# Splitting twenty weight tiles of a recurrent mixer beside the MLP before it, and a planner that knows two-operand reads

## Chip, cores and metric

One Trainium2 chip, one core. The metric is the device time of one execution in microseconds (us); lower is better.

## What is computed

Two layers over 1024 latent tokens and 256 context tokens, width 1024: banded attention with an MLP, then a recurrent block (a gated linear recurrence in two directions) with an MLP. Cut to what the change touches, the recurrent mixer is:

```python
w_gate, w_rec = w_in[:, :D_RNN], w_in[:, D_RNN:]             # D_RNN = 1280
u_x = centred_dwconv(h_x @ w_rec, conv_w, conv_b)            # and u_c for the context tokens
for d in range(2):                                           # both directions
    a_c, bx_c = rglru_coeffs(u_c, w_a[d], b_a[d], w_i[d], b_i[d], lam[d])
    ys_c, hc_last = linear_scan(a_c, bx_c, 0, rev, ...)
    a_x, bx_x = rglru_coeffs(u_x, w_a[d], b_a[d], w_i[d], b_i[d], lam[d])
    ys_x, _ = linear_scan(a_x, bx_x, hc_last, rev, True)
y_x = (gelu(h_x @ w_gate) * (rec_x[0] + rec_x[1])) @ w_out
```

`rglru_coeffs` multiplies `u`, in five blocks of 256 columns, with `w_a` and `w_i`, and takes sigmoid, exp, tanh and a square root of the products. All is fp32.

## The kernel before

**Products.** An fp32 product is made of three fp32r matmuls (`mm3`, lines 249 to 251): each operand is split into a high half (a copy rounded to fp32r) and a low half (the fp32 value minus the high half); high x high, high x low and low x high add up in PSUM. So each weight tile of 128x1024 goes through `plan_w`: a DMA into one of three `raw` buffers, a copy for the high half on ACT or DVE (line 244), a subtraction for the low half on DVE or POOL (line 1525, two SBUF inputs), both into one of four `w` slots; then `raw` is free again. A split is named by its output: `w` for whole tiles, `hw`, `ws` and `hc` for narrower ones.

**Stages.** Attention runs to about 660 us. The first MLP follows (`layer0_mlp`): after four columns of hidden units, fourteen steps of `plan_seven` make two tiles of hidden units each with seven products instead of eight, and put them in DRAM (`hid_d`, line 1447, 256 KB each). `plan_second` then reads them back and multiplies by `w2` in eight chunks of 2, 4, 4, 4, 4, 4, 4 and 2 tiles. Beside this run the rows of the conditioning vector (`plan_ada`, line 1236). `middle` plans the last four hidden tiles, the residual with its norms, the recurrent mixer and the start of the second MLP. `plan_in` makes the products of `w_in`: ten tiles for `u` (line 1883 begins their convolution; `u` goes to DRAM), and ten gate tiles, whose products of 512 tokens each run in two passes `g`, so each gate tile is loaded and split twice (ACT takes the gelu, line 1921). `plan_rec` runs for five blocks `n` and two directions: `u` is read back and split (`uh`, `uhc`, lines 1958 to 1967), the tile `wg[n, d]` is loaded and split, products `pg` follow, sigmoids (line 2005), exp, tanh and square root on ACT, products on DVE and POOL (lines 2047 to 2079), and scans on DVE (line 2087). The two directions are added (line 2120), multiplied by the gate (line 2123), put in DRAM and read back for the product with `w_out`.

**What sets the order.** `Plan` is a list scheduler that runs when the kernel is built. Every operation has one or several engines with a duration for each, a key (lower is more urgent), dependencies, and slots that it takes and frees (`w` 4, `raw` 3, `t` 32 places of 4 KB, `s` 21 places of 2 KB). `order` simulates the engines and emits each engine's instructions in the order of simulated time; `p.any` operations may go to DVE or POOL (or ACT), to the second engine only if it would end at most `alt` ns later than the first. All DMAs of this part are issued by SP in the order of their simulated times, so a DMA that waits holds those behind it. The layer-0 MLP and `middle` are one plan, with the keys `KEYS2`; the second MLP is another, with `KEYS3`.

Of the kernel before, what the change touches and what calls it, by code (L numbers as in the profile page):

```python
# [17 lines left out]
P = 128  # L18
D = 1024
# [23 lines left out]
class Plan:  # L43
# [14 lines left out]
    def add(self, eng, ns, key, fn, deps=(), take=(), free=(), tab=None):  # L58
# [23 lines left out]
    def order(self):  # L82
# [11 lines left out]
        bus = 0.0  # L94
# [19 lines left out]
        while len(at) < len(ops):  # L114
# [84 lines left out]
class Body:  # L199
# [190 lines left out]
    def run(self):  # L390
        tc, nc, A = self.tc, self.nc, self.A
        with ExitStack() as es:
# [18 lines left out]
            self.g_d = dt([4, 2, KT, P], F32, name="g_d")  # L411

# [741 lines left out]
    def layer0_mlp(self):  # L1154
# [58 lines left out]
        for c, n in enumerate([2] + [4] * 6 + [2]):  # L1213
            last = self.plan_second(p, l, 1000 + 100 * c, m, n, c, put, last, ys, yop, yh, (8, 9, 0, 1, 2, 3, 4, 5, 6, 7), rows)
            m += n
# [39 lines left out]

    def plan_ctx(self, p, key, j, z, o, zc, put):
# [34 lines left out]
    def plan_second(self, p, l, K, m, n, c, put, last, ys, yop, yh, order, rows=None, fin=False):  # L1291
# [14 lines left out]
        for i, t in enumerate(order):  # L1306
# [12 lines left out]
            if rows is not None and n == 4 and i in (1, 2, 3, 4, 5, 7, 8):  # L1319
                rows(1, K + 2 * i, o)  # L1320
            if fin:
# [290 lines left out]
    def plan_residual(self, p, key, t, ys, yop, xs, xop, G, put, norm):  # L1612
# [25 lines left out]
        for n in range(2):  # L1638
            g.append(p.any(PAIR(512), "DVE Pool", key, lambda e, n=n: e.tensor_tensor(
                out=y(n), in0=y(n), in1=G["G"][:, n * 512:(n + 1) * 512], op=ALU.mult), [sq[n], G["op"]]))  # L1640
            o.append(p.add("DVE", 665, key, lambda n=n: nc.vector.scalar_tensor_tensor(  # L1641
                out=x(n), in0=y(n), scalar=z["a"][:, 2:3], in1=x(n), op0=ALU.mult, op1=ALU.add), [r, g[n], xop]))
# [53 lines left out]
    def middle(self, p, ys, yop, yh, hput, last):  # L1696
# [58 lines left out]
        E["dep"] = last  # L1755
# [97 lines left out]
    def plan_in(self, p, E, h, hop, hold):  # L1853
# [5 lines left out]
        for m in range(NR):  # L1859
# [38 lines left out]
            for i in (0, 1, 3):  # L1898
                o = p.add("DVE", 1200, key, lambda i=i, z=z, tap=tap: tap(i, z["x"], z["u"]), [o], free=[(es[0], 0)] if i == 3 else [])
# [33 lines left out]
    def plan_rec(self, p, E):  # L1933
# [4 lines left out]
        for n in range(NB):  # L1938
# [32 lines left out]
            for kt in range(2):  # L1971
                lu.append(p.add("DMA", 2500, K - 4, load(kt), deps, take=["t"]))
                c = p.add("DVE", 800, K - 4, split_c(kt), [luc], take=["s"])
                a = p.add("DVE", 605, K - 4, split(kt, 0), [lu[kt]], take=["t"])
                b = p.add("DVE", 1140, K - 4, split(kt, 1), [a], take=["t"])
# [3 lines left out]
            for d in range(2):  # L1979
                K = Z["c0"] + (2 * n + d) * Z["cp"]  # L1980
                w = self.plan_w(p, A["wg"][n, d], K - 4, [gpe[-Z["bg"]] if gpe else E["dep"]], "DVE ACT")
# [49 lines left out]
                for jt in range(2):  # L2031
                    for c in (1, 0):
# [28 lines left out]
                        st[jt, c] = p.add("DVE", sz * 1.04 + 70, q, f_st, [b, w_], free=[(w_, 0)])  # L2061
# [7 lines left out]
                for jt in range(2):  # L2069
                    for c in (1, 0):  # L2070
# [11 lines left out]
                        bb[jt, c] = p.add("DVE", sz * 1.04 + 70, q, f_b, [x, iu[jt, c]], free=[] if c else [own["r%d" % jt]])  # L2082
# [9 lines left out]
                    x = p.add("DVE", 600, q, f_scan(0, 256, 1), [bb[jt, 1]])  # L2092
                    if d == 0:
                        x = p.add("DVE", 2130, q, f_scan(0, D, 0), [x, bb[jt, 0]], free=[own["a%d" % jt]])
                        sc[jt] = [x, x]
                    else:
                        x = p.add("DVE", 1140, q, f_scan(512, D, 0), [x, bb[jt, 0]])
                        sc[jt] = [p.add("DVE", 1140, q, f_scan(0, 512, 0), [x], free=[own["a%d" % jt]]), x]
# [115 lines left out]
```

## Time and profile before

| | us |
|---|---|
| median of three runs (2858.09 to 2860.35) | 2858.9 |
| the profiled execution | 2859.99 |
| its span, first to last instruction | 2858.2 |
| busy in the span: PE / DVE / ACT / POOL | 2673.9 / 2127.6 / 1107.5 / 851.0 |

The profile is one execution on the chip. PE is TensorE's matmuls, PEld its weight loads, DVE is VectorE, ACT is ScalarE, POOL is GpSimd, SP issues DMAs. Busy times of matmuls overlap, so that a full PE shows as 100% and the number of matmuls in a stretch tells its speed; the clock is given as the share of 2.4 GHz that was granted, which has a level of 1.2 GHz below it. The name behind a line is the tile written and those read. A wait row reads "who waits, at which tile and line <- what came last: us in total, times, longest".

### The profile page before, as it was taken

The numbers are of one execution on the slowest core, as the hardware profiler recorded it, in microseconds if no ns is written. First come the engines' busy times: TensorE is split into PE (matmuls) and PEld (weight loads), VectorE is DVE, ScalarE is ACT, GpSimd is POOL, SyncE is SP. The second block draws the span as 40 slices with busy tenths as digits, with TensorE's granted clock in tenths as the row PEclk, the third lists the DMA queues.
The fourth block names the chain that finished last, engine by engine and source line by source line (L and its number), as shares of the span: only waits on it lengthen the run. The fifth ranks groups of instructions, "written<-read, shape, count | busy, mean of one in ns | idle before, by whom it ended". The sixth has DMA issues, their size and how long they took to land. (4 is left out here: it accounts for less than half of the span.)

```text
span 2858.2 us, 35048 instructions
## 1 busy us (share of the span) xinstructions
PE 2673.9 (94%) x12886; PEld 2205.4 (77%) x12886; DVE 2127.6 (74%) x3178; ACT 1107.5 (39%) x2040; POOL 851.0 (30%) x720
## 2 busy tenths in 40 slices
PE   6798999998999999999998999978896999999997
PEld 4677788877788888888887887756675888888886
DVE  8988999996876666765668677799988666655546
ACT  5326777775322223111115245776525212221111
POOL 7643444443311110100116022355435111101113
PEclk9899999999999999999999999988998999999999
DMA  6462321224233334454552223334331323333323
GB/s 233 157 218 83 110 78 45 68 65 163 74 121 105 129 129 159 155 169 140 168 177 81 92 78 98 136 125 155 139 112 63 110 100 111 133 126 110 102 83 125
DMA packets 115332, 345.03 MB, mean 121 GB/s; under 512 B 12836, under 2 KB 15828, under 8 KB 115160
## 3 DMA queue, kind: packets, MB, share of 16 engines
q1 hardware_dynamic: 111704, 330.21, 34.2%
q10 hardware_dynamic: 3456, 12.58, 1.1%
q8 instruction: 101, 1.65, 0.2%
q14 instruction: 71, 0.58, 0.1%
HBM read 254.37 MB, written 88.38 MB: 120 GB/s over the span
## 5 line engine op out<-in xcount | busy, mean ns | idle before, releaser
L251 PE MATMUL pf<-h,w 128*128 128x512 f32 (+1 forms) x1400 | 517.5, 370 | 23.7 <-POOL w L1525 17.4
L250 PE MATMUL pf<-h,w 128*128 128x512 f32 (+1 forms) x1400 | 516.2, 369 | 9.8 <-DVE h L1593 9.5
L249 PE MATMUL pf<-h,w 128*128 128x512 f32 (+1 forms) x1400 | 516.6, 369 | 5.5 <-ACT h L1583 2.8
L1500 DVE TENSOR_TENSOR y<-y,py 128x512 f32<-128x512 f32 x268 | 183.0, 685 | 274.4 <-PE py L251 273.8
L251 PEld LDWEIGHTS pf<-h,w 128*128 128x128 f32 x1400 | 267.8, 191 | 70.5 <-POOL w L1525 20.0
L250 PEld LDWEIGHTS pf<-h,w 128*128 128x128 f32 x1400 | 267.8, 191 | 56.2 <-DVE h L1593 13.0
L249 PEld LDWEIGHTS pf<-h,w 128*128 128x128 f32 x1400 | 268.0, 191 | 50.7 <-ACT w L244 3.3
L244 ACT CAST w<-raw 128x1024 fp32r<-128x1024 f32 x142 | 148.4, 1049 | 325.2 <-PE pf L251 107.5
L249 PE MATMUL py<-hw,hw 128*128 128x512 f32 x592 | 230.4, 389 | 0.0
L251 PE MATMUL py<-hw,hw 128*128 128x512 f32 x592 | 230.3, 389 | 0.0
L250 PE MATMUL py<-hw,hw 128*128 128x512 f32 x592 | 230.3, 389 | 0.0
L244 ACT CAST hw<-raw 128x512 fp32r<-128x512 f32 x113 | 69.2, 621 | 391.3 <-DMA raw<-in_w 154.3
L1473 POOL TENSOR_TENSOR hw<-raw,hw 128x512 fp32r<-128x512 f32 x46 | 65.3, 1422 | 489.3 <-DVE hw L244 337.9
L1003 POOL TENSOR_SCALAR P<-P,sc 128x640 f32<-128x640 f32 (+2 forms) x160 | 118.5, 753 | 179.7 <-DVE sc L1000 92.2
L249 PE MATMUL py<-w,hw 128*128 128x512 f32 x432 | 169.0, 391 | 0.0
L250 PE MATMUL py<-w,hw 128*128 128x512 f32 x432 | 168.6, 390 | 0.0
L251 PE MATMUL py<-w,hw 128*128 128x512 f32 x432 | 168.4, 390 | 0.0
L1092 PE MATMUL py<-w,oT 128*128 128x512 f32 x480 | 147.5, 412 | 2.5 <-DVE w L927 1.8
L986 ACT ACTIVATE P<-S,sc 128x640 f32<-128x640 f32 (+2 forms) x160 | 113.9, 712 | 52.8 <-DVE sc L980 35.5
L1473 DVE TENSOR_TENSOR hw<-raw,hw 128x512 fp32r<-128x512 f32 x156 | 116.5, 769 | 20.1 <-ACT hw L244 18.4
L249 PEld LDWEIGHTS py<-hw,hw 128*128 128x128 f32 x592 | 111.1, 188 | 23.2
L251 PEld LDWEIGHTS py<-hw,hw 128*128 128x128 f32 x592 | 111.1, 188 | 23.1
(297 smaller groups left out, 6412.7 us busy)
## 6 DMA issues: line engine op xcount, KB each, us to landing
raw<-in_w SPq DMA_DIRECT2D x128, 512.0 KB, 3.5
raw<-in_ada_t SPq DMA_DIRECT2D x96, 512.0 KB, 3.8
raw<-hid_d SPq DMA_DIRECT2D x64, 512.0 KB, 4.0
hid_d<-c SPq DMA_DIRECT2D x112, 256.0 KB, 2.3
raw<-in_w_in SPq DMA_DIRECT2D x30, 512.0 KB
x<-x_d SPq DMA_DIRECT2D x26, 512.0 KB, 5.6
x_d<-x SPq DMA_DIRECT2D x24, 512.0 KB, 2.8
q_d<-qd ACTq DMA_DIRECT2D x20, 512.0 KB, 4.3
```

The source lines that it names most:

```text
L244: (e.copy if e is self.nc.scalar else e.tensor_copy)(out=out, in_=x)
L249: mm(o, lhsT=lh, rhs=rh, start=start, stop=False, skip_group_check=on)
L250: mm(o, lhsT=lh, rhs=rl, start=False, stop=False, skip_group_check=on)
L251: mm(o, lhsT=ll, rhs=rh, start=False, stop=stop, skip_group_check=on)
L986: nc.scalar.activation(out=z["P"][j][:, :n], in_=z["S", j][:, 256:256 + n], func=AF.Exp, scale=0.125, bias=negm[:, j:j + 1], accum_out=l[: ...
L1003: nc.gpsimd.tensor_scalar(out=z["P"][j][:, :n], in0=z["P"][j][:, :n], scalar1=z["sc"][3][:, j:j + 1], scalar2=1.0, op0=ALU.mult, op1=ALU.mult)
L1092: nc.tensor.matmul(z["ps", n], lhsT=oT[k // 2][2]["oT"][:, x, k % 2], rhs=Wo[k][:, w, n * 512:(n + 1) * 512], start=m == 0, stop=m == 3 * ...
L1473: e.tensor_tensor(out=z[n][:, 1], in0=z["raw"][:, s], in1=z[n][:, 0].bitcast(F32), op=ALU.subtract)
L1500: nc.vector.tensor_tensor(out=y, in0=y, in1=z["ps"], op=ALU.add)
```

## The change

- A new `plan_pre` splits the ten gate tiles of `w_in` and the ten tiles of `wg` in two halves of 512 columns each: per half a DMA in, a copy on ACT, a subtraction on DVE, and two DMAs that put the halves in a new DRAM tensor `ws_d`. One tile goes with each of the fourteen `plan_seven` steps and one with each of the six chunks of four in `plan_second`. It takes three `s` places per half.
- A new `plan_split` takes the place of `plan_w` for these tiles in the mixer: one DMA of 1 MB from `ws_d` straight into a `w` slot. That is twenty loads for the gates (each tile twice) and ten for `wg`. The ten `u` tiles of `w_in` and those of `w_out`, `w1` and `w2` stay with `plan_w`.
- The planner marks operations that read two SBUF operands. If POOL runs one of them, a marked DVE operation that starts meanwhile is simulated longer, by 0.3 of what is left of POOL's time, at most 0.43 of its own. DMAs over 4000 ns count twice on the simulated bus.
- All keys of `KEYS2` have new values. The first loads of `plan_in` wait for the third `w2` split instead of a matmul; the first `wg` load waits for the store of the second `u` tile.

```diff
@@ Plan.add
+    def add(self, eng, ns, key, fn, deps=(), take=(), free=(), tab=None, two=False):
...
+        if two or many and "Pool" in eng and "DVE" in eng:
+            self.two.add(len(self.ops))
@@ Plan.order
-            f = t + dict(opts)[eng]
-            if eng == "DMA" and dict(opts)[eng] >= 2000 and self.keys.get("bus"):
-                bus = max(t, bus) + self.keys["bus"] * (1 if dict(opts)[eng] > 2300 else 0.5)
+            d = dict(opts)[eng]
+            if i in self.two and self.cal:
+                if eng == "Pool":
+                    pool = t + d
+                elif eng == "DVE" and pool > t:
+                    d += min(0.43 * d, 0.3 * (pool - t))
+            f = t + d
+            if eng == "DMA" and key > -1e8 and d >= 2000 and self.keys.get("bus"):
+                bus = max(t, bus) + self.keys["bus"] * (2 if d > 4000 else 1 if d > 2300 else 0.5)
@@ KEYS2
-    KEYS2 = dict(m=(2.3, 0.68, 10.54), p=(7.5, 1.52, 9.72), h=(10.4, 11.24, 37.3), pi=0.66, a0=28.64, ap=9.33, al=-5.36, g0=155.5,
-                 g1=151.7, gp=4.73, c0=98.5, cp=2.33, w0=312.9, wp=16.6, r0=389.52, spill=5, tab=122.87, alt=72.5, ba=8, bb=6, bw=9, bg=7,
-                 bo=0, hm=1, cal=1, bus=2300, eps=dict(DVE=20, ACT=0, Pool=48))
+    KEYS2 = dict(m=(5.15, 1.46, -2.67), p=(-0.6, 0.76, 14.46), h=(21.62, 13.09, 34.46), pi=0.48, a0=28.13, ap=2.3, al=8.9, g0=118.63, g1=190.44,
+                 gp=4.47, c0=43.61, cp=4.66, w0=278.53, wp=17.22, r0=455.78, spill=5, tab=311.53, alt=600, ba=7, bb=8, bw=15, bg=5, bo=0, hm=1, cal=1,
+                 bus=2300, eps={'DVE': 20, 'ACT': 50, 'Pool': 0})
@@ layer0_mlp (and plan_second, for chunks of four: pre(1, K + 2 * i, o) at its first token tile)
+        pre = self.plan_pre(p)
...
+            pre(1, 100 + 20.0 * q + 8, pace[-1])
@@ new functions
+    def plan_pre(self, p):
+        left = [u for i in range(NR) for u in (("g", i), ("in", i))]
...
+                    def load(pool, hi, lo, z=z, u=u, s=s, tile=tile):
+                        z["raw"], z["pools"] = tile(pool), (hi, lo)
+                        nc.sync.dma_start(out=z["raw"], in_=src[u[0]](u[1])[:, s])
...
+                        nc.scalar.copy(out=z["hi"], in_=z["raw"])
...
+                        nc.vector.tensor_tensor(out=z["lo"], in0=z["raw"], in1=z["hi"].bitcast(F32), op=ALU.subtract)
...
+                        nc.sync.dma_start(out=self.ws_d[self.pre_at[u], :, i, s], in_=z[n].bitcast(F32))
+                    r = p.add("DMA", 2300, key, load, [dep], take=["s"] * 3)
+                    a = p.add("ACT", 630, key, f_hi, [r])
+                    b = p.add("DVE", 690, key, f_lo, [a], free=[(r, 0)])
+                    ops.append(p.add("DMA", 2300, key, lambda put=put: put("hi", 0), [a, b], free=[(r, 1)]))
+                    ops.append(p.add("DMA", 2300, key, lambda put=put: put("lo", 1), [b], free=[(r, 2)]))
...
+    def plan_split(self, p, u, key, deps=()):
...
+            z["w"] = self.wp.tile([P, 2, D], F32R, tag="w", name=self.name("w"))
+            self.nc.sync.dma_start(out=z["w"].bitcast(F32), in_=self.ws_d[self.pre_at[u]])
+        z["op"] = p.add("DMA", 5000, key, load, list(deps) + self.pre_op[u], take=["w"])
@@ middle, plan_in, plan_rec
-        E["dep"] = last
+        E["dep"] = w2[HW - 1]["op"]
...
-                w = self.plan_w(p, A["w_in"][m], key - 3, [back(Z["bb"])])
+                w = self.plan_split(p, ("in", m), key - 3, [back(Z["bb"])])
...
-                w = self.plan_w(p, A["wg"][n, d], K - 4, [gpe[-Z["bg"]] if gpe else E["dep"]], "DVE ACT")
+                w = self.plan_split(p, ("g", 2 * n + d), K - 4, [gpe[-Z["bg"]] if gpe else E["u", 1][0]])
```

## Rows read from the trace of the kernel before

**Rows 1.** The page's forty slices of the span: PE's busy tenths and its granted clock
```profile
PE   6798999998999999999998999978896999999997
...
PEclk9899999999999999999999999988998999999999
```

**Rows 2.** Windows: us; busy of PE, PEld, DVE, ACT, POOL; PE's clock; DMA share; GB/s
```profile
700.00:1100.00 400.00, 394.12 (x2070) 338.45 (x2069) 283.87 (x342) 104.48 (x161) 71.09 (x52) 1.00 0.34 116
1100.00:1500.00 400.00, 400.00 (x1773) 331.31 (x1773) 262.54 (x429) 67.45 (x113) 42.69 (x38) 1.00 0.48 159
1600.00:1680.00 80.00, 80.00 (x422) 69.09 (x421) 50.92 (x59) 17.47 (x27) 9.22 (x3) 1.00 0.27 97
1735.00:1980.00 245.00, 209.85 (x892) 169.44 (x891) 206.92 (x183) 165.62 (x219) 97.62 (x47) 0.91 0.39 132
1560.00:2140.00 580.00, 523.94 (x2380) 432.09 (x2381) 473.56 (x482) 304.47 (x436) 198.96 (x109) 0.94 0.34 117
2140.00:2220.00 80.00, 53.56 (x231) 42.82 (x230) 66.04 (x77) 40.46 (x72) 46.55 (x39) 0.83 0.17 65
```

**Rows 3.** Waits of PE, 1735 to 1980: us in total, times, longest
```profile
PE pf L251 <- POOL w L1525: 13.3, 5, 4.7
...
PE pg L249 <- DVE w L244: 4.6, 1, 4.6
...
PE pg L251 <- DVE w L1525: 2.1, 2, 1.7
PE pf L249 <- ACT w L244: 1.9, 2, 1.0
PE pf L251 <- DVE w L1525: 1.2, 1, 1.2
```

**Rows 4.** Tile raw, 1560 to 2010: the splits, their count and min/median/max ns
```profile
L1525 DVE TENSOR_TENSOR w<-raw,w x27: 1193/1218/3359, 1561.3 to 2003.6; 128x1024 fp32r<-128x1024 f32 x27
...
L244 DVE CAST w<-raw x15: 677/684/1787, 1571.5 to 2001.7; 128x1024 fp32r<-128x1024 f32 x15
L1525 POOL TENSOR_TENSOR w<-raw,w x13: 2354/3395/5599, 1572.3 to 1970.2; 128x1024 fp32r<-128x1024 f32 x13
```

**Rows 5.** Groups by line and shape, 1560 to 2140, DVE and POOL: busy us, mean ns
```profile
L1525 DVE TENSOR_TENSOR w<-raw,w 128x1024 fp32r<-128x1024 f32 x36 | 48.4, 1349 | 14.0 <-ACT w L244 13.8
...
L244 DVE CAST w<-raw 128x1024 fp32r<-128x1024 f32 x18 | 14.2, 790 | 0.0
...
L1525 POOL TENSOR_TENSOR w<-raw,w 128x1024 fp32r<-128x1024 f32 x14 | 51.5, 3682 | 140.0 <-ACT w L244 118.5 <-DVE w L244 11.6 <-issue 9.0
...
L2120 POOL TENSOR_TENSOR gi<-gi,gi 128x512 f32<-128x512 f32 x15 | 29.8, 2001 | 36.3 <-DVE gi L2087 21.3 <-DMA raw<-in_wg 15.0
```

**Rows 6.** Timeline, DVE and POOL, 1883 to 1899: start us, duration us
```profile
1883.53 2.40 POOL L2055 TENSOR_TENSOR gi<-gi,u 128x1024 f32<-128x1024 f32 x1 [0.42 <-ACT gi L2005]
...
1883.59 4.49 DVE L2087 TENSOR_TENSOR_SCAN gi<-ga,grc,gi 128x1024 f32<-128x1024 f32 x1
...
1897.86 2.34 DVE L2087 TENSOR_TENSOR_SCAN gi<-ga,grc,gi 128x1024 f32<-128x1024 f32 x1
```

**Rows 7.** Groups of ACT and DVE, 700 to 1500: the half-width splits there
```profile
L244 ACT CAST hw<-raw 128x512 fp32r<-128x512 f32 x54 | 33.2, 621 | 214.4 <-PE py L251 70.9 <-DMA raw<-in_w 69.0 <-DMA raw<-hid_d 55.2
...
L1473 DVE TENSOR_TENSOR hw<-raw,hw 128x512 fp32r<-128x512 f32 x79 | 59.3, 775 | 10.3 <-ACT hw L244 9.6
```

**Rows 8.** Waits, 700 to 1500, of SP, ACT and PE: us in total, times, longest
```profile
SPq L228 <- DVE hw L1473: 141.5, 41, 11.0
...
ACT hw L244 <- DMA raw<-in_w: 69.0, 10, 15.9
...
PE pf L251 <- DVE w L1379: 0.4, 1, 0.4
```

**Rows 9.** DMA issues by line: engine, count, KB each, median us from issue to landing
```profile
hid_d<-c SPq DMA_DIRECT2D x112, 256.0 KB, 2.3
...
x<-x_d SPq DMA_DIRECT2D x26, 512.0 KB, 5.6
```

More of the change, by code (lines that the diff above doesn't have):

```diff
@@ L55, in __init__ @@
         self.cal, self.base = keys.get("cal"), 0.0
-    def add(self, eng, ns, key, fn, deps=(), take=(), free=(), tab=None):
+        self.two = set()
+    def add(self, eng, ns, key, fn, deps=(), take=(), free=(), tab=None, two=False):
         many = not isinstance(eng, str)
@@ L93, in order @@
         tab = None
-        bus = 0.0
+        bus = pool = 0.0
         for i, o in enumerate(ops):
@@ L411, in run @@
             self.g_d = dt([4, 2, KT, P], F32, name="g_d")
+            self.ws_d = dt([2 * NR, P, 2, D], F32, name="ws_d")
             self.ident = cst.tile([P, P], F32, name="ident")
@@ L1213, in layer0_mlp @@
         for c, n in enumerate([2] + [4] * 6 + [2]):
-            last = self.plan_second(p, l, 1000 + 100 * c, m, n, c, put, last, ys, yop, yh, (8, 9, 0, 1, 2, 3, 4, 5, 6, 7), rows)
+            last = self.plan_second(p, l, 1000 + 100 * c, m, n, c, put, last, ys, yop, yh, (8, 9, 0, 1, 2, 3, 4, 5, 6, 7), rows, False, pre)
             m += n
@@ L1253, in plan_ada, with pre, tile, f_hi @@
         return rows
+    def plan_pre(self, p):
+        nc, A = self.nc, self.A
+        left = [u for i in range(NR) for u in (("g", i), ("in", i))]
+        src = {"in": lambda i: A["w_in"][i], "g": lambda i: A["wg"][i // 2, i % 2]}
+        self.pre_at = {u: i for i, u in enumerate(left)}
+        self.pre_op = {}
+        def pre(n, key, dep):
+            for _ in range(min(n, len(left))):
+                u = left.pop(0)
+                ops = self.pre_op[u] = []
+                for h in range(2):
+                    z = {}
+                    s = slice(h * 512, h * 512 + 512)
+                    def tile(pool, dt=F32):
+                        return pool.tile([P, 512], dt, tag="r", name=self.name("pw"))
+                    def load(pool, hi, lo, z=z, u=u, s=s, tile=tile):
+                        z["raw"], z["pools"] = tile(pool), (hi, lo)
+                        nc.sync.dma_start(out=z["raw"], in_=src[u[0]](u[1])[:, s])
+                    def f_hi(z=z, tile=tile):
+                        z["hi"] = tile(z["pools"][0], F32R)
+                        nc.scalar.copy(out=z["hi"], in_=z["raw"])
+                    def f_lo(z=z, tile=tile):
+                        z["lo"] = tile(z["pools"][1], F32R)
+                        nc.vector.tensor_tensor(out=z["lo"], in0=z["raw"], in1=z["hi"].bitcast(F32), op=ALU.subtract)
+                    def put(n, i, z=z, u=u, s=s):
+                        nc.sync.dma_start(out=self.ws_d[self.pre_at[u], :, i, s], in_=z[n].bitcast(F32))
[4 more added lines that the diff above has]
+                    ops.append(p.add("DMA", 2300, key, lambda put=put: put("lo", 1), [b], free=[(r, 2)]))
+        return pre
+    def plan_split(self, p, u, key, deps=()):
+        z = {}
+        def load():
+            z["w"] = self.wp.tile([P, 2, D], F32R, tag="w", name=self.name("w"))
+            self.nc.sync.dma_start(out=z["w"].bitcast(F32), in_=self.ws_d[self.pre_at[u]])
+        z["op"] = p.add("DMA", 5000, key, load, list(deps) + self.pre_op[u], take=["w"])
+        return z
     def plan_ctx(self, p, key, j, z, o, zc, put):
@@ L1288, in mlp, with plan_second @@
         p.emit(self.tc)
-    def plan_second(self, p, l, K, m, n, c, put, last, ys, yop, yh, order, rows=None, fin=False):
+    def plan_second(self, p, l, K, m, n, c, put, last, ys, yop, yh, order, rows=None, fin=False, pre=None):
         nc, A = self.nc, self.A
@@ L1320, in plan_second @@
                 rows(1, K + 2 * i, o)
+            if pre is not None and n == 4 and i == 0:
+                pre(1, K + 2 * i, o)
             if fin:
@@ L1641, in plan_residual @@
             o.append(p.add("DVE", 665, key, lambda n=n: nc.vector.scalar_tensor_tensor(
-                out=x(n), in0=y(n), scalar=z["a"][:, 2:3], in1=x(n), op0=ALU.mult, op1=ALU.add), [r, g[n], xop]))
+                out=x(n), in0=y(n), scalar=z["a"][:, 2:3], in1=x(n), op0=ALU.mult, op1=ALU.add), [r, g[n], xop], two=True))
         z["g"] = g
@@ L1898, in plan_in @@
             for i in (0, 1, 3):
-                o = p.add("DVE", 1200, key, lambda i=i, z=z, tap=tap: tap(i, z["x"], z["u"]), [o], free=[(es[0], 0)] if i == 3 else [])
+                o = p.add("DVE", 1200, key, lambda i=i, z=z, tap=tap: tap(i, z["x"], z["u"]), [o], free=[(es[0], 0)] if i == 3 else [], two=True)
             c = p.add("DVE", 1950, key, cc, [es[2]])
@@ L1973, in plan_rec @@
                 c = p.add("DVE", 800, K - 4, split_c(kt), [luc], take=["s"])
-                a = p.add("DVE", 605, K - 4, split(kt, 0), [lu[kt]], take=["t"])
-                b = p.add("DVE", 1140, K - 4, split(kt, 1), [a], take=["t"])
+                a = p.add("DVE", 605, K - 4, split(kt, 0), [lu[kt]], take=["t"], two=True)
+                b = p.add("DVE", 1140, K - 4, split(kt, 1), [a], take=["t"], two=True)
                 uop += [c, a, b]
@@ L2060, in plan_rec @@
                         ex[jt, c] = b
-                        st[jt, c] = p.add("DVE", sz * 1.04 + 70, q, f_st, [b, w_], free=[(w_, 0)])
+                        st[jt, c] = p.add("DVE", sz * 1.04 + 70, q, f_st, [b, w_], free=[(w_, 0)], two=True)
                         iu[jt, c] = p.any(PAIR(sz), "Pool DVE", q, f_iu, [sg[jt, 1, D]] if c else [sg[jt, 1, 0], sg[jt, 1, 512]])
@@ L2081, in plan_rec @@
                         x = p.add("ACT", sz * 0.833 + 93, q, f_sqrt, [st[jt, c]] + list(ex.values()), tab="sqrt")
-                        bb[jt, c] = p.add("DVE", sz * 1.04 + 70, q, f_b, [x, iu[jt, c]], free=[] if c else [own["r%d" % jt]])
+                        bb[jt, c] = p.add("DVE", sz * 1.04 + 70, q, f_b, [x, iu[jt, c]], free=[] if c else [own["r%d" % jt]], two=True)
                     def f_scan(lo, hi, c, jt=jt, view=view, sl=sl, d=d, t=t):
@@ L2091, in plan_rec @@
                     q = K + 3.5 + 0.3 * jt
[L2092 removed]
+                    x = p.add("DVE", 600, q, f_scan(0, 256, 1), [bb[jt, 1]], two=True)
                     if d == 0:
[L2094 removed]
+                        x = p.add("DVE", 2130, q, f_scan(0, D, 0), [x, bb[jt, 0]], free=[own["a%d" % jt]], two=True)
                         sc[jt] = [x, x]
                     else:
[L2097 to L2098 removed]
+                        x = p.add("DVE", 1140, q, f_scan(512, D, 0), [x, bb[jt, 0]], two=True)
+                        sc[jt] = [p.add("DVE", 1140, q, f_scan(0, 512, 0), [x], free=[own["a%d" % jt]], two=True), x]
                 p.when([sc[0][0], sc[1][0]], [own["rc0"], own["rc1"], own["ac"]])
```

## Prediction

> **What bounds the kernel now.** I read three things in this order: the forty slices of the span, then the windows by stage, then what TensorE waited for in the worst stage. In the slices PE is at 9 tenths nearly everywhere, and the dips that come with a lower granted clock lie near the start, near slice 21 and in slices 26 to 30 [rows 1]. The windows tell the stages apart [rows 2]. The first MLP is bound by PE: 394 and 400 us busy of 400, clock 1.00, DVE at 284 and 263. The mixer, 1560 to 2140, is not: of 580 us PE is idle 580 - 523.9 = 56 us, and a clock of 0.94 costs about 0.06 x 580 = 35 us more. That is some 91 us of loss. It is not spread evenly: from 1600 to 1680 PE loses nothing and DVE is busy only 51 of 80 us; from 1735 to 1980 PE is idle 35 us, the clock is 0.91, and DVE is busy 207 of 245 us. After it, 2140 to 2220, PE waits for the residual and norm of the last tokens (26 us idle, clock 0.83).
>
> Which input came last in the worst stretch is told by the list of waits [rows 3]: TensorE waited 13.3 us for the low half of a gate weight from POOL, 1.2 and 2.1 us for the same from DVE, 4.6 and 1.9 us for the high half. Together 23.1 of its 35 idle us end at the split of a weight tile. By then the last recurrent input tile is through, so these are tiles of the two kinds that the change treats.
>
> **What the change removes.** Thirty splits of 128x1024 tiles in the mixer: ten gate tiles of `w_in`, twice each, and ten tiles of `wg`. From 1560 to 2010 there are 40 splits: 27 low halves on DVE, 13 on POOL, 15 high halves on DVE, the other 25 on ACT [rows 4]; 30 of these 40 go. At three quarters, with the means of the mixer [rows 5]: DVE loses 20 x 1.35 + 11 x 0.79 = 36 us, POOL 10 x 3.68 = 37 us. That is 36 of the 474 us that DVE is busy in the mixer [rows 2].
>
> What the path gets back I take from the waits, not from the busy time. Idle time: 23.1 us. Clock: 245 x 0.09 = 22 us are lost in that stretch; the windows without idle time keep 1.00 and those with it don't [rows 2] (0.91 is 18% of the stretch at 1.2 GHz instead of 2.4), so I give the splits the same share, 23.1 / 35.2 x 22 = 14.5 us. Sum 37.6, taken as 38 us. The bounds: nothing, if another input is late at the same moments; and 91 - 20 = 71 us, if the freed DVE and POOL time ends the mixer's other stops too and only the 12 idle us of this stretch that end elsewhere stay, with their 8 us of clock.
>
> **What it adds in the first MLP.** Twenty units in two halves each: 40 high halves on ACT at 0.62 us = 25 us, 40 low halves on DVE at 0.78 us = 31 us [rows 7], and 120 DMAs of 256 KB on SP, 40 in and 80 out. DVE then stands at 284 + 263 + 31 = 578 of 800 us, ACT at 172 + 25 = 197 [rows 2]. The traffic is 20 x 1.5 MB = 31 MB over some 700 us, 45 GB/s on top of 116 to 159, with the DMA engines 0.34 to 0.48 busy [rows 2]. I cost it at nothing, because PE covers it: in these 800 us PE waited 0.4 us for a split weight in all, though ACT itself waited 69 us in 10 pieces for weights to land [rows 8]. If the cover goes, the price is the stall itself. The puts add waits to SP's queue: each waits for ACT or DVE, and the next raw weight stands behind it. SP already waits 3.5 us on average for a low half of DVE (141.5 in 41) [rows 8].
>
> **What it adds in the mixer.** A load of 1 MB now lands straight in one of the four `w` slots, and waits on SP for TensorE to leave a slot; the stores of `u` and `ge` and the loads of `u` stand behind it. No row shows 1 MB. The bounds are 2.3 us, as 256 KB, and 11.2 us, twice the slowest 512 KB [rows 9]; I take 6, near that 5.6 us row. A gate tile feeds PE for 24 x 0.226 = 5.4 us (1773 matmuls fill 400 us [rows 2]), so three other slots cover 16 us. I cost it at nothing; uncovered, each late tile costs up to 6 us, 30 of them more than everything gained.
>
> **What it moves.** The new keys start the recurrence earlier (`c0` 98.5 to 43.6) and the recurrent input tiles closer together (`ap` 9.33 to 2.3), which brings DVE work forward to where 29 of 80 us are unused (1600 to 1680 [rows 2]). It also raises `alt` from 72.5 to 600 ns, so the planner gives more to POOL. The first input tiles wait for a split of `w2` instead of a matmul, which can shift the mixer's first products by a few us either way. The stop at 2140 to 2220 depends on the keys too; a quarter of its 26 idle us gives 7 us either way. I take these at zero and keep 8 us for the range.
>
> **The sum.** The profiled execution took 2859.99 us (span 2858.2); 2860 - 38 = 2822, and the median of the runs shown stands 1.1 us lower: 2821 us.
>
> **A rule that speaks against a part.** First the rows: POOL began a two-input multiply at 1883.53 for 2.40 us; a scan that DVE took up at 1883.59 lasted 4.49 us, against 2.34 us for the same scan at 1897.86 [rows 6]. The excess, 2.15 us, is nearly all that was left of POOL's operation (2.34 us). The changed planner charges 0.3 of that, 0.7 us, and nothing to POOL. The Trainium skill says the same as the row (SBUF — State Buffer, "Who interferes with whom"): the pair of ports that DVE and GpSimd share is an exclusive lock, so that the one who comes second is blocked and not merely slowed. By that rule the planner still thinks POOL too cheap, and the trace agrees. What that would make of the time is the second rival.
>
> **The rivals.** *The wait changes its name.* The splits ended the waits, but gate products, `uh` halves or the landing of the 1 MB tile come as late. For it: DVE is 84% busy in the stretch, 12 of the 35 idle us end elsewhere already. Against: the split is the latest of all inputs in 11 cases [rows 3]. Half of the 38 us is lost: 2840 us.
>
> *POOL fills up again.* With `alt` at 600 ns the 37 us freed on POOL are given to 512-wide operations at 2.00 us (18 of them [rows 5]); each saves DVE some 0.7 us (half of the 1.35 us for 1024 [rows 5]) and blocks it for up to 2.0 us. Net 18 x 1.3 = 23 us back: 2844 us.
>
> *The whole mixer evens out.* DVE at 474 - 36 = 438 us lies below PE's 580 - 91 = 489 us, so PE could bound the stage if the order is good: 2860 - 71 - 1 = 2788 us.
>
> *Nothing moves.* The chain conv, split, gates, scan, output sets the mixer's length, whatever the weights do: 2854 to 2864 us. For it: from 1735 to 1980 DVE is 84% busy, mostly with work that stays [rows 2]. Against: PE, not DVE, is what the splits stopped.
>
> *Slower, through SP's queue in the first MLP.* Each of the 20 units puts six DMAs in SP's one queue; if its puts hold the next `w1`, `w2` or `hid_d` load for the 3.5 us of [rows 8] and TensorE feels it, that is 20 x 3.5 = 70 us: 2891 us. It decides from 38 / 20 = 1.9 us for each unit. Against it: weights already land late for ACT by 6.9 us on average without stopping PE [rows 8]; so there is slack of that order.
>
> **How the numbers follow.** Forecast 2821: 0.38. The wait changes its name: 0.17. POOL fills up: 0.10. The mixer evens out: 0.12. Nothing moves: 0.08. Slower: 0.15. A measurement here can tell about 0.2%, 6 us, from no change; so faster 0.77, same 0.08, slower 0.15. The range goes from 2788 (half of the evened-out case lies below) to 2865 (most of the slower case lies above).
>
> **What would show it.** Right: in the mixer's waits the rows of PE for `w` from POOL or DVE are gone or belong to the ten recurrent and ten output tiles; idle time there falls from 56 to about 30 us and the clock rises above 0.96; the first MLP stays at 400 of 400. Wrong: PE waits for the DMA of `ws_d` in the mixer, POOL's busy time there is still about 200 us with longer scans, or PE drops below 394 and 400 in the first MLP.

## The result, and the profile after

The changed kernel takes 2808.3 us (median of four runs, 2807.4 to 2809.8) against 2859.6 us before (four runs, 2858.1 to 2862.8): 0.982 of the time, interval 0.9803 to 0.9837, 51 us less. The forecast was 2821 us. The profiled execution took 2807.43 us, its span is 2805.7 us. Two executions, one of the kernel before and the profiled one of the full lock below, ran at a clock of 0.84 where all others have 0.97 to 0.98, took 3042 and 3028 us, and are left out of every comparison.

Windows of the changed kernel, columns as in [rows 2]. The last line but one is the mixer at its new place, and the last the start of the stop behind it.

```profile
700.00:1100.00 400.00, 394.32 (x2047) 337.45 (x2046) 299.44 (x363) 122.05 (x194) 81.04 (x58) 1.00 0.50 166
1100.00:1500.00 400.00, 400.00 (x1788) 331.70 (x1788) 257.20 (x402) 73.31 (x129) 78.91 (x67) 1.00 0.57 185
1600.00:1680.00 80.00, 80.00 (x422) 69.04 (x421) 49.86 (x60) 28.31 (x41) 10.74 (x4) 1.00 0.28 98
1735.00:1980.00 245.00, 230.74 (x1048) 190.09 (x1047) 197.85 (x188) 182.84 (x251) 94.07 (x48) 0.96 0.55 196
1560.00:2105.00 545.00, 507.17 (x2388) 422.74 (x2387) 413.00 (x436) 299.81 (x436) 171.96 (x103) 0.96 0.44 153
2105.00:2180.00 75.00, 63.11 (x288) 51.84 (x287) 71.00 (x69) 40.70 (x75) 60.99 (x47) 0.91 0.20 77
```

The first MLP is as full as it was: 394 and 400 us of 400. In the bad stretch, 1735 to 1980, PE's idle time fell from 35.2 to 14.3 us, its clock rose from 0.91 to 0.96, and it began 1048 matmuls instead of 892. In the whole mixer idle time fell from 56 to 38 us. And the stop behind the mixer has a clock of 0.91 instead of 0.83. What lies on either side of that stretch, before and then after:

```profile
1560.00:1735.00 175.00, 168.39 (x857) 144.35 (x858) 126.30 (x140) 66.93 (x98) 35.28 (x15) 0.96 0.26 91
...
1980.00:2140.00 160.00, 145.69 (x635) 118.29 (x634) 140.34 (x161) 71.92 (x119) 66.06 (x48) 0.96 0.36 124
```

```profile
1560.00:1735.00 175.00, 174.18 (x910) 149.58 (x909) 109.79 (x131) 59.01 (x89) 20.96 (x11) 1.00 0.37 126
...
1980.00:2105.00 125.00, 102.25 (x434) 83.07 (x433) 105.36 (x118) 57.96 (x98) 56.93 (x44) 0.89 0.31 107
```

The end of the mixer, from 1980 on, got worse: PE is idle there for 22.8 us instead of 14.3, in a shorter stretch and at a lower clock.

What PE waited for from 1735 to 1980, columns as in [rows 3], the whole answer:

```profile
PE py L260 <- DVE w L1590: 4.9, 3, 2.3
PE pg L259 <- DMA w<-ws_d: 4.1, 1, 4.1
PE pg L260 <- DVE uh L2025: 4.0, 3, 1.7
PE py L259 <- DVE w L254: 0.5, 1, 0.5
PE pg L259 <- DVE uh L2023: 0.4, 1, 0.4
PE py L259 <- ACT w L254: 0.3, 1, 0.3
```

Of the waits of [rows 3] for gate tiles (`pf`) and for tiles of `wg` (`pg`) none is left. What still waits for a split is `py`, the output product, whose weights were left to the mixer. One wait has the cause that the prediction named as the one to fear, a 1 MB load from `ws_d`: 4.1 us, once. The wider stretch 1560 to 2140 has two larger rows, and both lie after 1980:

```profile
PE py L259 <- DVE y L1746: 22.7, 4, 12.4
PE pf L260 <- POOL h L1658: 4.9, 2, 4.2
```

Before, the output products waited for `y` too, but half as long; before, the same stretch:

```profile
PE py L249 <- ACT y L1679: 9.7, 3, 5.7
...
PE py L249 <- DVE y L1681: 1.7, 1, 1.7
```

Where do the 52.5 us between the two spans lie? I cut both traces at the same three events in PE's timeline: the first product of the first `u` tile (start of the mixer), the last output product `py<-w,z` (its end), and the first product of the second MLP's second stage (`py<-hw,hw`). What lies between the last two I call the stop, since PE has nearly the same work in it in all kernels here: 1368 products and the transposes before them. Without idle time and at full clock this takes an estimated 313 us (326 us busy before, at a clock of 0.96), and the rest of its length is loss. Where an expectation below says that the stop or the mixer "loses" time, it means such a loss.

| | before | after | difference |
|---|---|---|---|
| start of the mixer | 1548.0 | 1547.4 | -0.6 |
| length of the mixer | 592.6 | 558.3 | -34.3 |
| length of the stop | 352.5 | 334.5 | -18.0 |
| from there to the end of the span | 365.1 | 365.5 | +0.4 |

So two things happened: 34 us in the mixer, where the prediction put 38, and 18 us in the stop, where it put zero.

### The profile page after: what moved, and what is told of

Its sections match the earlier page's. It is cut to its first block, busy times and chain, and to the rows that moved or that the text cites. A ratio compares the mean times of both kernels' runs of the same rounds, so it can differ in the third digit from the quotient of the medians.

```text
span 2805.7 us, 35386 instructions
## 1 busy us (share of the span) xinstructions
PE 2654.4 (95%) x12886; PEld 2194.4 (78%) x12886; DVE 2072.5 (74%) x3088; ACT 1130.3 (40%) x2105; POOL 899.1 (32%) x767
## 4 chain that ended last, share of the span: by engine, by line
PE 68%; DVE 13%; POOL 4%; ACT 4%; issue 3%; DMA 2%; SPq 0%; DVEq 0%; ACTq 0%; POOLq 0%
PE pf L261 10%; PE pf L259 10%; PE pf L260 10%; PE py L260 9%; PE py L261 9%; PE py L259 9%; PE py L1103 2%; PE tp L1020 1%; DVE x L1706 1%; PE pv L1034 1%; DVE sc L990 1%; PE pg L260 1%; PE pg L259 1%; PE pg L261 1%; DVE gi L2152 1%
## 5 line engine op out<-in xcount | busy, mean ns | idle before, releaser
L260 PE MATMUL pf<-h,w 128*128 128x512 f32 (+1 forms) x1400 | 511.3, 365 | 5.9 <-POOL h L1658 5.6
L261 PE MATMUL pf<-h,w 128*128 128x512 f32 (+1 forms) x1400 | 511.3, 365 | 4.1 <-DVE w L1444 3.1
L259 PE MATMUL pf<-h,w 128*128 128x512 f32 (+1 forms) x1400 | 512.0, 366 | 1.6 <-ACT hf L1653 1.6
L260 PEld LDWEIGHTS pf<-h,w 128*128 128x128 f32 x1400 | 265.1, 189 | 48.6 <-POOL h L1658 6.8
L261 PEld LDWEIGHTS pf<-h,w 128*128 128x128 f32 x1400 | 264.8, 189 | 48.1 <-DVE w L1444 3.9
L259 PEld LDWEIGHTS pf<-h,w 128*128 128x128 f32 x1400 | 265.1, 189 | 44.7 <-ACT hf L1653 2.0
L1538 POOL TENSOR_TENSOR hw<-raw,hw 128x512 fp32r<-128x512 f32 x78 | 109.4, 1408 | 580.5 <-DVE hw L254 306.7
L254 ACT CAST w<-raw 128x1024 fp32r<-128x1024 f32 x126 | 131.9, 1049 | 320.0 <-PE pf L261 107.5
L259 PEld LDWEIGHTS py<-hw,hw 128*128 128x128 f32 x592 | 111.1, 188 | 23.2
L260 PEld LDWEIGHTS py<-hw,hw 128*128 128x128 f32 x592 | 111.1, 188 | 23.1
L261 PEld LDWEIGHTS py<-hw,hw 128*128 128x128 f32 x592 | 111.1, 188 | 23.0
```

The source lines that it names most:

```text
L254: (e.copy if e is self.nc.scalar else e.tensor_copy)(out=out, in_=x)
L259: mm(o, lhsT=lh, rhs=rh, start=start, stop=False, skip_group_check=on)
L260: mm(o, lhsT=lh, rhs=rl, start=False, stop=False, skip_group_check=on)
L261: mm(o, lhsT=ll, rhs=rh, start=False, stop=stop, skip_group_check=on)
L1538: e.tensor_tensor(out=z[n][:, 1], in0=z["raw"][:, s], in1=z[n][:, 0].bitcast(F32), op=ALU.subtract)
```

## Experiments

Each run is compared with runs of the kernel before on the same chip. Lengths are those of the table above, from one profiled execution each; its time is up to 4 us off the median. The theory: the splits carry the mixer's gain. The rivals: the keys do it by a better order, or the planner does, because it knows about two-operand reads.

**Only the work taken away, the order kept.** In the kernel before, the low halves of the thirty tiles are cut to 16 columns, and the matmuls read the high half in their place (`z["e"]` is 0 for these tiles), so the low half of these weights is left out.

```diff
-            e.tensor_tensor(out=z["w"][:, 1], in0=z["raw"], in1=z["w"][:, 0].bitcast(F32), op=ALU.subtract)
+            s = slice(0, c or D)
+            e.tensor_tensor(out=z["w"][:, z["e"], s], in0=z["raw"][:, s], in1=z["w"][:, 0, s].bitcast(F32), op=ALU.subtract)
...
+                w = self.plan_w(p, A["w_in"][m], key - 3, [back(Z["bb"])], c=16)
```

> The kernel before with its order of instructions kept; the low halves of the thirty tiles (gates of w_in, wg) are made for 16 columns only and TensorE reads the high half twice, so the low parts of these weights are left out of the result. About 20 DVE subtractions and 10 on POOL shrink, some 27 and 37 us of busy time. If the splits were what stopped TensorE: 2820 to 2838 us, and its waits for w from POOL and DVE in the mixer fall from 29 us to under 10. If other inputs are as late at the same moments: 2850 us or more.

Measured: 2832.6 us, ratio 0.9907 (0.9891 to 0.9922). The mixer takes 566.3 us, 26 less; the stop 352.3 us, as before. No order changed, so these 26 us are the price of the low halves' work alone, with the high halves and the old order still there. The second part of the expectation missed: PE's waits for `w` from POOL and DVE, in the rows `pf` and `pg` of the mixer, fell from 28.8 to 20.7 us and not under 10. In this run the short subtraction writes into the high half, so that the first product waits for its place in the queue. The waits for `gp`, `grc`, `uh` and `y` fell as well, from 22.7 to 14.1 us together. So what the splits cost is more than the waits that end at a split: their work also makes other inputs late.

**Only the keys.** The kernel before with the new `KEYS2`, with no early splits and no charge.

```diff
-    KEYS2 = dict(m=(2.3, 0.68, 10.54), p=(7.5, 1.52, 9.72), h=(10.4, 11.24, 37.3), pi=0.66, a0=28.64, ap=9.33, al=-5.36, g0=155.5,
+    KEYS2 = dict(m=(5.15, 1.46, -2.67), p=(-0.6, 0.76, 14.46), h=(21.62, 13.09, 34.46), pi=0.48, a0=28.13, ap=2.3, al=8.9, g0=118.63, g1=190.44,
...
```

> The kernel before with the new values of KEYS2 and nothing else: no tile is split early, no charge for two operands. If the gain comes from the splits that are gone: 2845 to 2870 us. If it comes from the new order alone: 2808 to 2825 us. The stop after the mixer (38 us lost before, 15 to 21 after) tells whether the keys shorten it without the early splits.

Measured: 2837.9 us, ratio 0.9922 (0.9906 to 0.9937), between the two expectations. The mixer gained only 8 us (584.5); 15.5 us came from the stop (337.0). The keys work mostly elsewhere than I had looked.

**The change without the early splits**, with all keys, the charge and the new dependencies.

```diff
-        pre = self.plan_pre(p)
+        pre = lambda *a: None
...
-                w = self.plan_split(p, ("in", m), key - 3, [back(Z["bb"])])
+                w = self.plan_w(p, A["w_in"][m], key - 3, [back(Z["bb"])])
...
-                w = self.plan_split(p, ("g", 2 * n + d), K - 4, [gpe[-Z["bg"]] if gpe else E["u", 1][0]])
+                w = self.plan_w(p, A["wg"][n, d], K - 4, [gpe[-Z["bg"]] if gpe else E["u", 1][0]], "DVE ACT")
```

> The changed kernel without the early splits: keys, charge and dependencies are new, the thirty tiles are split in the mixer as before. Theory of the splits: 2840 to 2860 us, with TensorE waiting 20 us or more for w in the mixer. Theory of the planner: under 2825 us.

Measured: 2838.6 us, ratio 0.9924 (0.9909 to 0.994). Mixer 590.2 us, as before; stop 336.1 us, as after. The window of the bad stretch in this kernel:

```profile
1735.00:1980.00 245.00, 204.21 (x881) 166.65 (x880) 217.59 (x182) 176.58 (x235) 128.09 (x58) 0.90 0.39 131
```

PE is no better off than before (204 busy, 881 matmuls), and POOL has 128 us of work where the changed kernel has 94. The mixer's gain is gone with the splits and the stop's is not: the two are separate. The time lies just under the range of the theory of the splits. Against "Only the keys" this run adds the charge and the new dependencies, and the two times agree: without early splits these bring nothing.

**The change with the old keys**, early splits and charge kept.

```diff
-    KEYS2 = dict(m=(5.15, 1.46, -2.67), p=(-0.6, 0.76, 14.46), ...
+    KEYS2 = dict(m=(2.3, 0.68, 10.54), p=(7.5, 1.52, 9.72), ...
```

> The changed kernel with the old values of KEYS2: early splits, the charge and the new dependencies stay. If the splits that are gone bring the gain whatever the order: 2815 to 2835 us. If it takes the new keys to use the freed time: 2845 us or more. If the keys brought the 18 us of the stop after the mixer, that stop is at 35 us or more again.

Measured: 2840.1 us, ratio 0.9926 (0.9908 to 0.9943), between the two expectations. Mixer 568.2 us, stop 349.7 us, and the mixer starts 8 us late (1555.9). The first MLP lost them. PE's waits in it, 700 to 1560, and its first window:

```profile
PE pf L259 <- DVE c L1497: 5.5, 4, 3.4
```

```profile
700.00:1100.00 400.00, 389.93 (x2012) 333.05 (x2011) 290.66 (x364) 116.31 (x182) 67.13 (x48) 0.99 0.48 162
```

PE waits for DVE's work on the hidden columns and falls to 389.9 us. ACT and DVE ahead of the longest of these waits, 3.4 us until 771.18:

```profile
769.18 1.26 ACT L1293 CAST pw<-pw 128x512 fp32r<-128x512 f32 x2 [10.72 <-DMA pw<-in_wg]
```

```profile
769.83 0.69 DVE L1297 TENSOR_TENSOR pw<-pw,pw 128x512 fp32r<-128x512 f32 x1 [4.03 <-ACT pw L1293]
770.44 0.68 DVE L1497 TENSOR_TENSOR c<-c,pf 128x512 f32<-128x512 f32 x1
```

The add that PE waits for stands in DVE's queue behind the low half of an early split (`pw`). That waits for ACT's copy, and the copy for the load of the early split itself. DVE stands idle in the same way ahead of two of the other three waits, 2.6 and 2.4 us. So the cover of the early splits holds for some orders only, and what broke it here was an early split whose own load came late, with work of the first MLP behind it in the queues.

**Early splits alone**: with the old keys and no charge; the new dependencies stay.

```diff
-                    d += min(0.43 * d, 0.3 * (pool - t))
+                    pass
```

and `KEYS2` of before.

> The early splits and the new dependencies alone: old keys, no charge. The same with the charge took 2840 us. If the splits that are gone carry the mixer's gain by themselves: the mixer from its first product to its last loses 24 to 32 us less than the 99 of before, the stop behind it still loses 36 us or more, and the time is 2830 to 2845 us. If they need the charge: above 2848 us.

Measured: 2813.9 us, ratio 0.984 (0.9824 to 0.9857). Mixer 551.2 us, 41 less than before; stop 350.3 us; start 1548.1, so the first MLP pays nothing here. That is 16 us below the range that was expected if the splits carry the mixer's gain: the mixer gained 41 us where 24 to 32 were expected, and the first MLP did not lose its 8. The early splits alone give 45 us, where the whole change gives 51. Against the run above, the charge alone turned 2814 into 2840 us.

**No charge for two operands**, the rest as changed (the same line replaced by `pass`).

> The changed kernel with the charge for two-operand reads set to zero: DVE operations that meet POOL are simulated at their plain length; early splits and keys stay. If what the planner knows of the shared port is part of the gain: 2815 to 2835 us. If early splits and keys bring it all: 2803 to 2813 us.

Measured: 2805.7 us, ratio 0.9815 (0.9801 to 0.983), which can't be told from the changed kernel. What the planner was taught of two operands is worth nothing here. The double count of long DMAs stayed in every run with early splits, so what it is worth is not shown.

**The full lock in the planner.** Now both engines wait for what is left of the other's two-operand work.

```diff
                 if eng == "Pool":
+                    d += max(0.0, dve - t)
                     pool = t + d
-                elif eng == "DVE" and pool > t:
-                    d += min(0.43 * d, 0.3 * (pool - t))
+                elif eng == "DVE":
+                    d += max(0.0, pool - t)
+                    dve = t + d
```

> The changed kernel with a planner that makes the second of a DVE and a POOL operation, both marked, wait for the whole rest of the first, in both directions, instead of 0.3 of it on DVE alone. If POOL is thought too cheap and that costs time: 2785 to 2803 us, with POOL under 150 us busy in the mixer and shorter scans. If the order has enough slack for the error, or the keys fit the old charge: 2803 to 2830 us.

Measured: 2825.0 to 2833.5 us (median 2829.0), ratio 0.9897 (0.988 to 0.9913). A planner that lets each engine block the other makes a kernel some 20 us slower than the changed one, with keys that belong to the lighter charge. Why it is slower is not shown.

**What shortens the stop?** Three runs on the kernel before or the changed one. First `alt` alone in the kernel before, 72.5 to 600 ns:

```diff
-                 g1=151.7, gp=4.73, c0=98.5, cp=2.33, w0=312.9, wp=16.6, r0=389.52, spill=5, tab=122.87, alt=72.5, ba=8, bb=6, bw=9, bg=7,
+                 g1=151.7, gp=4.73, c0=98.5, cp=2.33, w0=312.9, wp=16.6, r0=389.52, spill=5, tab=122.87, alt=600, ba=8, bb=6, bw=9, bg=7,
```

> The kernel before with alt at 600 ns instead of 72.5 and nothing else. If it is the free choice of a second engine that shortens the stop after the mixer: that stop loses under 25 us instead of 39, and the time is 2835 to 2850 us. If it is the other keys: the stop stays at 36 us or more, and the time is 2850 us or more; with POOL busier in the mixer it may be above 2865 us.

Measured: 2851.5 us, ratio 0.9975 (0.9964 to 0.9986), a little above the range. The stop is 327.6 us, 24.9 shorter; the mixer is 605.5 us, 12.9 longer, and starts 3.5 us later. Part of this only moved across the cut between the two: 28 of the 64 transposes that begin the stop run before the mixer's end here. Then the keys of the last stage alone (`w0`, `wp`, `r0`) in the kernel before:

```diff
-w0=312.9, wp=16.6, r0=389.52
+w0=278.53, wp=17.22, r0=455.78
```

> The kernel before with the new values of w0, wp and r0 alone, the keys of the output product and of the residual and norm behind it. If these shorten the stop after the mixer: it loses under 25 us instead of 39, the mixer itself is unchanged, and the time is 2838 to 2848 us. If not: the stop stays above 36 us and the time within 6 us of 2860.

Measured: 2857.5 us, ratio 1.0002 (0.9992 to 1.0011); stop 352.7 us. They do nothing. Last, `alt` back to 72.5 ns in the changed kernel without its charge, against "No charge" above:

```diff
-                 ... tab=311.53, alt=600, ba=7, ...
+                 ... tab=311.53, alt=72.5, ba=7, ...
```

> The changed kernel without the charge for two operands, as in e4, and with alt back at 72.5 ns; every other key is new. If it is alt alone that shortens the stop behind the mixer (as it did in the kernel before, by 24.9 us), the stop goes from 335.5 us back to about 352, and the mixer, which alt lengthened by 12.9 us there, may shorten by as much: 2806 + 17 - (0 to 13) = 2810 to 2823 us. If the other new keys carry the stop (rival), it stays at 335 us and the time is 2793 to 2806 us.

Measured: 2810.7 us, ratio 0.9829 (0.9813 to 0.9845). Stop 349.2 us instead of 335.5, mixer 549.7 us instead of 554.3. So `alt` carries the stop with early splits too, and pays for part of it in the mixer. The times tell less than the lengths: the medians lie 5 us apart, and the two intervals overlap. How, stands in PE's timeline behind the mixer's end. In this kernel (end 2098.6; columns are start, duration, what, and the idle time before it):

```profile
2105.56 0.48 PE L1644 MATMUL ph<-ident,y 128*128 128x128 f32 x1 [6.93 <-DVE y L1720]
2111.42 0.47 PE L1644 MATMUL ph<-ident,y 128*128 128x128 f32 x1 [5.39 <-ACT y L1718]
2114.26 0.48 PE L1644 MATMUL ph<-ident,y 128*128 128x128 f32 x1 [2.36 <-ACT y L1718]
2117.70 7.21 PE L1644 MATMUL ph<-ident,y 128*128 128x128 f32 x49 [2.97 <-ACT y L1718]
2124.93 0.50 PE L259 MATMUL pf<-h,w 128*128 128x512 f32 x1
```

And in the changed kernel (end 2105.7):

```profile
2105.51 2.78 PE L1644 MATMUL ph<-ident,y 128*128 128x128 f32 x24
2109.83 0.66 PE L1644 MATMUL ph<-ident,y 128*128 128x128 f32 x4 [1.54 <-DVE hf L1655]
...
2114.97 0.80 PE L260 MATMUL pf<-h,w 128*128 128x512 f32 x1 [4.25 <-POOL h L1658]
...
2138.48 2.78 PE L1644 MATMUL ph<-ident,y 128*128 128x128 f32 x24
```

With `alt` at 72.5 ns 52 of the 64 transposes of the normed rows, of all eight token tiles, stand in PE's queue ahead of the first product of the second MLP, and PE waits 17.6 us for the last rows. In the changed kernel 28 stand there, of the first four tiles, whose rows are nearly all ready at the mixer's end; the first products follow, and the other four tiles are normed beside them. The thirteen traces with lengths in the table below agree: the eight kernels with a stop of 349 to 359 us have 44 to 52 transposes in front and 17.6 to 23.4 us of idle time at them; the five with 327 to 337 us have at most 32, and at most 4.4 us. So I take PE's order to decide, and `alt` to be what tipped it here; no run changed that order alone.

**Can both be had?** In the changed kernel PE's largest wait is `py <- DVE y`. The adds of the output products (`y`, line 1746) stand in DVE's queue behind scans. First all of them are made urgent, then those of the first three blocks only:

```diff
-                yo[n] = p.add("DVE", 605, key, put_y, [o, yo[n]], free=["mm"])
+                yo[n] = p.add("DVE", 605, key - 400, put_y, [o, yo[n]], free=["mm"])
```

> The changed kernel with one key changed: the additions of the output products to y on DVE (L1746) are 400 more urgent, so that they no longer stand behind the scans. In the changed kernel TensorE waits 22.7 us in 4 pieces for them. If that order is the new bound of the mixer: 2780 to 2800 us. If the scans that are put off become late instead: 2805 to 2815 us.

```diff
+                yo[n] = p.add("DVE", 605, key - soon, put_y, [o, yo[n]], free=["mm"])
...
+                             yh, 400 if n < NB - 2 else 0)
```

> The changed kernel, with the additions of the output products to y made 400 more urgent for the blocks 0 to 2 alone; the last two blocks, which the stop behind the mixer hangs on, keep their keys. If the stop was what the urgent additions cost before (24 us more there, 5 us less in the mixer): the stop stays near 21 us lost and the time is 2790 to 2806 us. If any change of these keys upsets the stop: above 2815 us.

Measured: 2827.3 us, ratio 0.989 (0.9876 to 0.9905), and 2816.4 us, ratio 0.9851 (0.9837 to 0.9866). The mixer did get shorter, 553.3 and 546.0 us, but the stop went to 358.7 and 356.4 us: PE's order fell back to 48 transposes in front, with `alt` still at 600. The first is slower than either of its expectations; the second came out where the expectation has it if any change of these keys upsets the stop. Neither beats the changed kernel. A kernel with the mixer of the last one and the stop of the changed one would be 12 us faster than it (558.3 - 546.0); no run here has both.

| | time, us | mixer | stop |
|---|---|---|---|
| before | 2859 | 592.6 | 352.5 |
| low halves cut, order kept | 2832.6 | 566.3 | 352.3 |
| keys alone | 2837.9 | 584.5 | 337.0 |
| changed, no early splits | 2838.6 | 590.2 | 336.1 |
| changed, old keys | 2840.1 | 568.2 | 349.7 |
| early splits alone | 2813.9 | 551.2 | 350.3 |
| changed, no charge | 2805.7 | 554.3 | 335.5 |
| the same with `alt` 72.5 | 2810.7 | 549.7 | 349.2 |
| `alt` alone | 2851.5 | 605.5 | 327.6 |
| last keys alone | 2857.5 | 589.5 | 352.7 |
| changed, `y` urgent | 2827.3 | 553.3 | 358.7 |
| changed, early `y` urgent | 2816.4 | 546.0 | 356.4 |
| changed, full lock | 2829.0 | not read | not read |
| changed | 2808.3 | 558.3 | 334.5 |

## Why the prediction was right, and where it was not

**The splits that go, 38 us: right in kind, and in size partly by luck.** The mixer is 34.3 us shorter. The counts came close as well; tile `raw`, 1560 to 2010, as in [rows 4]:

```profile
L1590 DVE TENSOR_TENSOR w<-raw,w x10: 1215/1226/2290, 1559.2 to 1958.0; 128x1024 fp32r<-128x1024 f32 x10
...
L254 DVE CAST w<-raw x4: 681/694/694, 1596.0 to 1923.7; 128x1024 fp32r<-128x1024 f32 x4
L1590 POOL TENSOR_TENSOR w<-raw,w x4: 2399/3018/3367, 1629.8 to 1995.2; 128x1024 fp32r<-128x1024 f32 x4
```

DVE lost 17 low and 11 high halves (forecast 20 and 11), POOL 9 (forecast 10). The two parts of the sum came out as idle time 56.1 to 37.8 us, 18.3 less (forecast 23.1), and clock 0.06 x 580 = 35 to 0.04 x 545 = 22 us, 13 less (forecast 14.5). But each is a difference of two larger numbers. From 1560 to 1980 idle time fell from 41.8 to 15.1 us, 27 less, and the clock's loss from 0.04 x 175 + 0.09 x 245 = 29 to 0.04 x 245 = 10 us, 19 less: 46 us, more than the 38. From 1980 on the waits for `y` and a clock of 0.89 took some 8 and 7 us of the two back. That it is the splits, and not the keys, the runs show from both sides: 26 us with the low halves cut and nothing else changed, 41 us for the early splits alone, 32 us between the changed kernel with and without them. Whether waits or busy time should be summed these numbers can't tell: the prediction put DVE's lost busy time at 36 us, which is as near. That the clock falls just where PE is idle was read too simply: from 700 to 1100 it keeps 1.00 with 5.9 us idle [rows 2]. The term is no constant either: it goes from 26 to 41 us with the order around it and with what is taken away.

**The stop at zero, 8 us either way: wrong.** This is the step that failed. It was read as 26 us of idle time, of which "a quarter" could move. I had named what PE waited for there, the residual and norm of the last tokens, but did not ask why PE needed these rows so soon. PE's waits before, 2140 to 2240:

```profile
PE ph L1579 <- ACT y L1653: 8.2, 1, 8.2
PE ph L1579 <- POOL y L1655: 7.6, 2, 4.7
...
PE ph L1579 <- DVE y L1655: 2.0, 1, 2.0
```

These 17.8 us stand at transposes, which hold up PE because its queue has those of all eight tiles before the first product. A change in the planner's simulated times can turn that order over, and then most of this idle time goes, with the clock's share: 18.0 us here, 14 to 25 us by `alt` in the runs. With 34.3 in place of 38 and 18.0 in place of 0 the sum is 2860 - 52 = 2808 us for the profiled execution, which took 2807.43.

**The additions in the first MLP at zero: right with these keys.** ACT did 23 us more than before in the two windows (forecast 25). DVE did 10 us more, 556.6 us in all (forecast 578), since POOL took over low halves of other tiles: its two windows went from 113.8 to 160.0 us. PE waited 4.0 us for split weights there (`w` and `ws`), against 0.4 before [rows 8]. Its waits for other inputs fell by as much, so that its idle time stayed at 6 us:

```profile
PE pf L261 <- POOL ws L1444: 2.7, 1, 2.7
PE pf L259 <- ACT hf L1653: 1.6, 1, 1.6
PE pf L261 <- DVE w L1444: 0.8, 1, 0.8
PE pf L259 <- ACT ws L254: 0.5, 1, 0.5
```

The slower rival, through SP's queue, did not come: loads do land later for ACT, whose copies `hw` now wait 77.9 us in 11 pieces for `raw<-in_w` (69.0 in 10 before) and 132.7 us in 22 for `raw<-hid_d` (55.2 in 15), but ACT still runs ahead of PE. Where the MLP did lose, 8 us with the old keys and the charge, the way was another than this rival's: the load that came late was that of an early split, and it held the MLP's own work behind it in the queues of ACT and DVE.

**The 1 MB loads at zero: right.** The page's list of DMA issues (KB each, us to landing):

```profile
w<-ws_d SPq DMA_DIRECT2D x30, 1024.0 KB, 6.2
...
ws_d<-pw SPq DMA_DIRECT2D x80, 256.0 KB, 2.9
```

6.2 us against 6 taken. The Trainium skill states 6.15 us for 1 MB (DMA: Bandwidth & Descriptors, "Measured (HBM→SBUF, 128 partitions, SWDGE, issued from GpSimd)"). The trace comes near it, but it is not the same quantity: the page gives the busy span of the DMA engines for a DMA issued from GpSimd, the row the time from issue to landing on SP's queue. One load of thirty was late by the time that PE noticed, 4.1 us.

**The wait changes its name: in part.** `py` waits 22.7 us for DVE's `y` in four pieces, where it waited 11.4 us for `y` of ACT and DVE before. It is no split that became another input of the same product, as the rival had it; it is a later stage that now runs among the scans. The same row has 20.3 us with the keys alone and 17.5 with the splits alone. Without the charge it has 19.8 us in a mixer of 554 us, and with `alt` back at 72.5 ns 9.2 us in one of 550 us: a short mixer does not have to bring this wait. `alt` is part of its cause; the rest is not shown. DVE and POOL ahead of the longest piece, 12.43 us until 2005.47:

```profile
1993.99 4.43 DVE L2152 TENSOR_TENSOR_SCAN grc<-gac,grc 128x256 f32<-128x256 f32 x2
1998.35 6.48 DVE L2152 TENSOR_TENSOR_SCAN gi<-ga,grc,gi 128x1024 f32<-128x1024 f32 x2
2004.76 4.36 DVE L1746 TENSOR_TENSOR y<-y,py 128x512 f32<-128x512 f32 x7
```

```profile
1992.93 2.26 POOL L2220 TENSOR_TENSOR z<-zb,z 128x512 fp32r<-128x512 f32 x1 [4.36 <-ACT z L254]
1995.16 2.72 POOL L1590 TENSOR_TENSOR w<-raw,w 128x1024 fp32r<-128x1024 f32 x1
1997.84 4.84 POOL L2220 TENSOR_TENSOR z<-zb,z 128x512 fp32r<-128x512 f32 x2
```

Seven adds stand behind four scans. Two scans of 256 columns took 4.43 us beside POOL's work; the same pair took 1.27 us at 2038.80. The two of 1024 took 6.48 us, against 2 x 2.34 for the one that ran alone before [rows 6]. That is 3.16 + 1.80 = 5.0 us of the 12.43.

**POOL fills up: no.** POOL's busy time in the mixer fell from 199 to 172 us though `alt` allows it more; it took 19 of the 512-wide operations `gi<-gi,gi` instead of 15. The rule behind that rival, that the second one of DVE and GpSimd is blocked and not slowed (the Trainium skill, SBUF — State Buffer, "Who interferes with whom"), agrees with the excess of the scans above. The time that the rival made of it did not come: neither the lighter charge (2805.7 without it, 2808.3 with it) nor the full lock (2825 to 2834) bought anything with these keys. *The mixer evens out* did not come either: 38 idle us are left in it, more than the 30 that were named as a sign of being right, and the clock is 0.96, not above it.

## What to carry to other kernels

The waits of the bound engine that end at the work to be taken away give the size of what can be won, but other inputs are late by the same work, and later stages can take a part back, as `y` did here. Ask of every other wait on the list whether it has a cause in the data or only in the order of a queue: a wait of the second kind can vanish or come back with a retuning, as the stop did here, so it belongs in the range at its full size. When parts of a change are timed alone, expect that they don't add: here the keys alone gave 22 us, the early splits alone 45, and both together, without the charge, 53. Work moved beside a stage that another engine fills is free only as long as the order there holds; the same early splits under the same old keys cost nothing without the planner's charge, and 8 us with it.

## What was not expected

- A list scheduler's order is touchy. A cost for a real effect made the kernel 26 us slower with the old keys (2813.9 to 2840.1 us) and some 20 us slower as the full lock; no operation was added or taken away in either case.
- One number, `alt`, at the same time shortened the stop by 14 to 25 us and lengthened the mixer by 5 to 13 us, as cut here. Seen from the total alone (7 us in the kernel before, 5 us with early splits) it looks like a weak parameter.
- Thirty loads of 1 MB took the mixer's traffic from 117 to 153 GB/s and its DMA share from 0.34 to 0.44, and yet the 512 KB reloads of `x` landed sooner in the median, 4.5 us instead of 5.6 [rows 9]. Why, no run here tells.
